# Scan products of a hybrid encoder: x stationary in half of the array, the decay matrix moving, the result transposed back

## The chip, the core and the metric

The kernel runs on one core of a Trainium2 chip, as one launch. The metric is the device time of that launch in microseconds (us), the median of several runs. A profiled execution gives the trace that is read here. TensorE is called PE in the rows, its weight loads PEld, VectorE DVE, ScalarE ACT, GpSimd POOL, and SyncE, which issues the DMAs, SP.

## What is computed

Two layers of an encoder over 256 positions of width 1024. Each layer has three parts: a mixer with three branches (dilated window attention, a state-space scan in both directions, a Fourier mix) whose outputs are gated, summed and projected; cross-attention into 256 memory tokens; and a SwiGLU feed-forward. The change touches the scan. Per head, with 32 heads of 64 channels in 4 groups, the reference has in essence

```
a_cs   = cumsum(dt * a)                              # per head, over positions
lmat   = exp(where(tri, a_cs[l] - a_cs[s], -inf))    # decay from s to l
cb     = einsum('bclgn,bcsgn->bcgls', C, B)
y_diag = einsum('bcgls,bcgels,bcsgep->bclgep', cb, lmat, x * dt)
y      = y_fwd + y_bwd + x * d_skip
```

For each head the diagonal part is a matrix over positions (cb times decays, both directions) times that head's x, 64 columns wide.

## The kernel before

Weights stream from memory in pieces of 1 MB, in the order of a list (`ORDER` and what follows it). SP loads a piece, ACT rounds it to a high part `wh` (L327), DVE takes the rest `wl` (L328), and PE multiplies three products per weight tile (L357 to L359, 512 columns moving; L418 to L420, 256 columns moving). There are three buffers each of raw and split pieces. After a piece, `done()` splits the piece three further on, and `pump()` gives background tasks some credit.

All else is background: Python generators in seven lanes, in which each `yield` ends a step. A step's yielded number is its price in credit; `LATER` blocks its lane for four pumps, `SOON` for three; a tuple such as `4, 0` says how many 4 KB and 2 KB slots of on-chip memory must be free before the next step. `drain()` runs everything that is left. A scheduler then orders each engine's instructions.

The scan of a group is `ssd_group`: two tiles (`tt`, 128 positions each) of eight heads. A tile fetches the cumulative sums of both directions from memory, spread over all partitions (`s<-dd`), builds `E` for eight heads (L841, L842, L848) and the weights `W` (L844, L845), multiplies them (L852), and scales x into `Xo` and `Xo2` (L862, L864). After `LATER` come eight products (L869) into the bank `pd`, with one head's 128x128 block of `E` stationary and 64 columns of x moving, and one product `po` (L870) for the other half of the positions. DVE adds and scales (L872 to L874), and the slots of `E` come free. With 2 layers, 4 groups and 2 tiles there are 16 such tiles, so 128 instructions at L869. The scan's output is then gated and normed (`ssd_gate`) and transposed (L907).

The list order is: Fourier, B and C columns, x, q, k, v, z columns mixed with gate columns, the attention branch (token BA, which waits for the attention lane), the last gate columns (G1), then `drain()`, then the projection of the scan's output (`branch(fl(yT), 4, ...)`), which uses group 0's output first and group 3's last.

Of the kernel before, what the change touches and what calls it, by code (L numbers as in the profile page):

```python
# [17 lines left out]
P = 128  # L18
# [15 lines left out]
LATER, SOON = "later", "soon"  # L34
# [141 lines left out]
def trunk(ctx: ExitStack, tc: tile.TileContext, a, out):  # L176
    nc = tc.nc
    V, A, T, G = nc.vector, nc.scalar, nc.tensor, nc.gpsimd
# [19 lines left out]
    def slot(size, shape, dt):  # L198
        keep = 0 if running[0] else RESERVE
        while len(slots[size]) <= keep and step():  # L200
            pass
        if not slots[size]:
            raise RuntimeError(f"no slot of {size} KB")
        r = slots[size].popleft()
        t = r.tile(shape, dt, name=nm("s%d_" % size))
        owner[id(t)] = (size, r, t)
        return t

    def s4(shape, dt=F32):
        return slot(4, shape, dt)  # L210

    def s2(shape, dt=F32):
        return slot(2, shape, dt)

    def free(*ts):
        for t in ts:
            if isinstance(t, (tuple, list)):
                free(*t)
            else:
                size, r, _ = owner.pop(id(t))  # L220
                slots[size].append(r)
# [4 lines left out]
    def banks_of(pool, n, p):  # L226
        banks = deque(pool.tile([P, 512], F32, name=f"{p}{i}") for i in range(n))

        def f():
            banks.rotate(-1)  # L230
            return banks[-1]
        return f

    tp = banks_of(pst, 4, "tp")
# [15 lines left out]
    def step(only=None, force=True):  # L250

        if running[0]:
            return False
        for k in (list(turn) if only is None else [only]):
            q = lanes[k]
            if blocked[k] and not force or need[k][0] > len(slots[4]) or need[k][1] > len(slots[2]):
                continue
            need[k] = (0, 0)
            while q:
                running[0] = True  # L260
                try:
                    c = next(q[0])
                except StopIteration:
                    q.popleft()
                    continue
                finally:
                    running[0] = False
                if isinstance(c, tuple):
                    need[k] = c
                elif c in (LATER, SOON):  # L270
                    blocked[k] = WAIT if c is LATER else NWAIT if k == "n" else XWAIT
                    if not force:
                        break
                else:
                    credit[0] -= c
                turn.remove(k)
                turn.append(k)
                return True
        return False
# [11 lines left out]
                raise RuntimeError("a background task waits for slots")  # L291

    def drain():
        while step():
            pass
        if any(lanes.values()):
            raise RuntimeError("a background task waits for slots")
        credit[0] = 0.0
# [53 lines left out]
    def ordered():  # L352

        return tc.manual_schedule(engines={mybir.EngineType.PE})
# [75 lines left out]
    def const(name, shape, src, dt=F32, eng=None):  # L430
        t = cp.tile(shape, dt, name=name)
        (eng or nc.sync).dma_start(t, src)
        return t
# [4 lines left out]
    idn = const("idn", [P, P], a["c_idn"])  # L438
# [382 lines left out]
    def ssd_group(l, g, xT, R, Dbc, ys):  # L821

        dt, nacs, wof, el = R["dt"], R["nacs"], R["wof"], R["el"]
        cbd, off = R["cb", g]
        yield 1, 0
        y = ys[g] = s4([P, 2, 512])
        for tt in range(2):
            yield 4, 0
            bcs = []
            for hf in range(2):  # L830
                b = s4([P, 4, 2, P])
                nc.sync.dma_start(b, bass.AP(tensor=R["dd"].tensor,
                                             offset=R["dd"].offset + (8 * g + 4 * hf) * 512 + tt * P,
                                             ap=[[0, P], [512, 4], [S, 2], [1, P]]))
                bcs.append(b)
            E = s4([P, 8, P])
            W = s4([P, 8, P])
            for j in range(8):
                hf = 8 * g + j
                b = bcs[j // 4][:, j % 4]  # L840
                A.activation(E[:, j, :], b[:, 1, :], AF.Identity, bias=nacs[:, tt, 32 + hf:33 + hf])  # L841
                V.scalar_tensor_tensor(E[:, j, :], b[:, 0, :], nacs[:, tt, hf:hf + 1], E[:, j, :],  # L842
                                       op0=ALU.add, op1=ALU.min)
                A.activation(W[:, j, :], cbd[:, tt, 0, :], AF.Copy, scale=dt[:, tt, hf:hf + 1])  # L844
                V.scalar_tensor_tensor(W[:, j, :], cbd[:, tt, 1, :], dt[:, tt, 32 + hf:33 + hf], W[:, j, :],  # L845
                                       op0=ALU.mult, op1=ALU.add)
                if j % 4 == 3:
                    A.activation(E[:, j - 3:j + 1, :], E[:, j - 3:j + 1, :], AF.Exp)  # L848
                    yield 1.6
            for hf in range(2):  # L850
                hs = slice(4 * hf, 4 * hf + 4)
                V.tensor_mul(E[:, hs, :], E[:, hs, :], W[:, hs, :])  # L852
            free(bcs, W)
            yield 1.1

            d = 1 - tt
            sl = slice(8 * g, 8 * g + 8)
            v8 = lambda t: t.rearrange("p (a b) -> p a b", a=8)
            bc8 = lambda t: t[:, :, None].to_broadcast([P, 8, 64])
            yield 0, 2  # L860
            Xo = s2([P, 512])
            V.tensor_mul(v8(Xo), v8(xT[:, 1 - tt, :]), bc8(wof[:, d, sl]))  # L862
            Xo2 = s2([P, 512])
            V.tensor_mul(v8(Xo2), v8(xT[:, tt, :]), bc8(Dbc[:, sl]))  # L864
            yield 1.2
            yield LATER
            pd, po = tp(), tp()
            for j in range(8):
                T.matmul(pd[:, j * 64:(j + 1) * 64], E[:, j, :], xT[:, tt, j * 64:(j + 1) * 64], start=True, stop=True)  # L869
            T.matmul(po, off[:, tt, :], Xo, start=True, stop=True)  # L870
            yt = y[:, tt, :]
            V.tensor_add(yt, Xo2, pd)  # L872
            V.tensor_mul(v8(Xo), v8(po), bc8(el[:, tt, sl]))
            V.tensor_add(yt, yt, Xo)  # L874
            free(E, Xo, Xo2)
            yield 1.8
        free(cbd, xT)
        if g == 3:
            free(R["off"])
# [132 lines left out]
    for l in range(L):  # L1012
# [104 lines left out]
        for n, tok in enumerate(ORDER):  # L1117
            k, g = tok[0], int(tok[1]) if tok[1].isdigit() else 0
# [20 lines left out]
            elif k == "x":  # L1139
                xT = s4([P, 2, 512])  # L1140
# [19 lines left out]
            elif tok == "BA":  # L1160
                drain_until(lambda: "oT" in R and R.get("a"), "a")
                branch(fl(R["oT"]), 1, ga)
                free(R["oT"], ga)
        free(h)
        drain()
        mT = ftiles(2)

# [312 lines left out]
```

## Time and profile before

| what | us |
|---|---|
| median of 3 runs | 1613.19 (1612.34 to 1613.2) |
| the profiled execution's own time | 1612.18 |
| its span, first to last instruction | 1610.1 |
| PE busy | 1592.1 |
| weight loads busy | 1381.0 |
| DVE busy | 1163.8 |
| ACT busy | 956.5 |

The profiled execution took 2.1 us outside the span of its instructions. A matmul in full 32-bit floats leaves two records in the trace, each with its own weight load; a transpose or a matmul on rounded operands (fp32r) leaves one. The time from one record's start to the next's (the pitch) tells what a matmul costs in a stream; its recorded duration holds the latency as well, which overlaps with the next.

### The profile page before, as it was taken

Reading aid. Unit: us, or ns where it says so; the run is one execution under the profiler, and the core shown is the slowest. Engines: PE = TensorE matmul, PEld = TensorE weight load, DVE = VectorE, ACT = ScalarE, POOL = GpSimd, SP = SyncE. Lnnn points to the kernel's source line nnn. Section 1 sums busy time; section 2 is a strip of 40 time slices with the busy share of each in tenths; the row PEclk is TensorE's granted clock in tenths of the full one; section 3 lists DMA queues with packets and bytes.
Section 4 is the critical chain, followed back from the end, with each engine's and each line's share of the span. In section 5 each row is a group of like instructions: output and inputs, shape, how many; then the busy total and the mean of one; then the engine's idle time right before and its main releaser. Section 6 shows DMA issues by size and latency. Waiting matters only on the chain.

```text
span 1610.1 us, 22777 instructions
## 1 busy us (share of the span) xinstructions
PE 1592.1 (99%) x8994; PEld 1381.0 (86%) x8994; DVE 1163.8 (72%) x1777; ACT 956.5 (59%) x1587; POOL 43.8 (3%) x47
## 2 busy tenths in 40 slices
PE   8999999999999999999999999999999999999999
PEld 6998888888887888999889888888888878889997
DVE  5999997889757566555478999978886576565543
ACT  5666868787445664444356678677964457554442
POOL 0000000000000100000000000000100001000000
PEclk9999999999999999999999999999999999999999
DMA  8446655455556444555554577455555545345552
GB/s 298 159 161 230 223 182 181 167 196 192 196 196 223 177 153 162 198 183 184 183 190 146 182 230 242 154 189 179 172 185 203 202 181 196 131 169 175 183 190 95
DMA packets 84579, 299.46 MB, mean 186 GB/s; under 512 B 7305, under 2 KB 46857, under 8 KB 52728
## 3 DMA queue, kind: packets, MB, share of 16 engines
q1 hardware_dynamic: 84472, 298.01, 52.8%
q8 instruction: 70, 1.15, 0.3%
q14 instruction: 37, 0.30, 0.1%
HBM read 296.77 MB, written 1.22 MB: 185 GB/s over the span
## 4 chain that ended last, share of the span: by engine, by line
PE 91%; DVE 4%; ACT 2%; DMA 1%; POOL 1%; issue 1%; SPq 0%; DVEq 0%; ACTq 0%; POOLq 0%
PE acc L358 20%; PE acc L357 20%; PE acc L359 20%; PE acc L418 7%; PE acc L419 7%; PE acc L420 7%; PE tp L869 1%; PE tp L477 1%; PE tp L357 1%; PE tp L359 1%; PE tp L358 1%; PE tp L619 1%; DVE wl L328 1%; PE tp L940 1%; ACT wh L327 1%; PE tp L870 1%
## 5 line engine op out<-in xcount | busy, mean ns | idle before, releaser
L328 DVE TENSOR_TENSOR wl<-wr,wh 128x2048 fp32r<-128x2048 f32 (+1 forms) x256 | 572.6, 2239 | 278.5 <-ACT wh L327 277.9
L327 ACT CAST wh<-wr 128x2048 fp32r<-128x2048 f32 (+1 forms) x256 | 477.6, 1867 | 387.8 <-PE acc L359 184.3
L357 PE MATMUL acc<-wh,s 128*128 128x512 f32 x1520 | 604.4, 398 | 0.1
L358 PE MATMUL acc<-wl,s 128*128 128x512 f32 x1520 | 599.6, 395 | 1.6 <-DVE wl L328 1.6
L359 PE MATMUL acc<-wh,s 128*128 128x512 f32 x1520 | 596.2, 393 | 0.0
L358 PEld LDWEIGHTS acc<-wl,s 128*128 128x128 f32 x1520 | 288.0, 189 | 61.7 <-DVE wl L328 3.9
L357 PEld LDWEIGHTS acc<-wh,s 128*128 128x128 f32 x1520 | 287.9, 189 | 59.3 <-issue 1.4
L359 PEld LDWEIGHTS acc<-wh,s 128*128 128x128 f32 x1520 | 287.8, 189 | 58.0 <-issue 0.4
L418 PE MATMUL acc<-s,wh 128*128 128x256 f32 x960 | 273.3, 285 | 0.0
L419 PE MATMUL acc<-s,wh 128*128 128x256 f32 x960 | 271.7, 283 | 0.0
L420 PE MATMUL acc<-s,wl 128*128 128x256 f32 x960 | 271.6, 283 | 0.0
L418 PEld LDWEIGHTS acc<-s,wh 128*128 128x128 f32 x960 | 184.1, 192 | 1.1 <-issue 0.7
L419 PEld LDWEIGHTS acc<-s,wh 128*128 128x128 f32 x960 | 184.2, 192 | 0.8 <-issue 0.5
L420 PEld LDWEIGHTS acc<-s,wl 128*128 128x128 f32 x960 | 184.1, 192 | 0.0
L710 DVE SCALAR_TENSOR_TENSOR s<-s,cw,s 128x254 f32<-128x254 f32 (+2 forms) x288 | 120.9, 476 | 0.3
L841 ACT ACTIVATE s<-s,nacs 128x128 f32<-128x128 f32 x128 | 46.4, 392 | 13.4 <-DVE s L852 5.6
L844 ACT ACTIVATE s<-s,dt 128x128 f32<-128x128 f32 x128 | 45.3, 394 | 0.0
L842 DVE SCALAR_TENSOR_TENSOR s<-s,nacs,s 128x128 f32<-128x128 f32 x128 | 42.4, 344 | 3.5 <-ACT s L841 3.5
L845 DVE SCALAR_TENSOR_TENSOR s<-s,dt,s 128x128 f32<-128x128 f32 x128 | 41.5, 343 | 0.0
L493 DVE TENSOR_TENSOR s<-tp,s 128x512 fp32r<-128x512 f32 x56 | 36.9, 683 | 5.3 <-ACT s L492 5.2
L1199 DVE TENSOR_TENSOR X<-X,acc 128x512 f32<-128x512 f32 x24 | 16.4, 684 | 27.9 <-PE acc L359 27.9
L461 ACT ACTIVATE s<-X 128x512 f32<-128x512 f32 x24 | 15.1, 630 | 35.6 <-DVE X L1199 33.4
(224 smaller groups left out, 1418.8 us busy)
## 6 DMA issues: line engine op xcount, KB each, us to landing
wr<-in_wstream SPq DMA_DIRECT2D x248, 1024.0 KB, 4.8
s<-dd SPq DMA_DIRECT2D x32, 512.0 KB, 5.1
s<-in_wstream SPq DMA_DIRECT2D x6, 512.0 KB, 3.3
s<-vd SPq DMA_DIRECT2D x12, 256.0 KB, 5.9
wr<-in_wstream SPq DMA_DIRECT2D x8, 256.0 KB, 5.3
s<-in_ssd_norm_g SPq DMA_DIRECT2D x8, 256.0 KB, 3.2
s<-in_memT SPq DMA_DIRECT2D x4, 512.0 KB, 6.4
X<-in_x SPq DMA_DIRECT2D x2, 512.0 KB, 3.6
```

Of the source, the lines that this page charges most:

```text
L327: A.copy(hi[:, c], raw[:, c])
L328: V.tensor_sub(lo[:, c], raw[:, c], hi[:, c].bitcast(F32))
L357: T.matmul(o, sh, mh, start=start, stop=False)
L358: T.matmul(o, sh, ml, start=False, stop=False)
L359: T.matmul(o, sl, mh, start=False, stop=stop)
L418: T.matmul(o, hi[:, w0:w0 + P], sh[:, k, :], start=kt == 0, stop=False)
L419: T.matmul(o, hi[:, w0:w0 + P], sl[:, k, :], start=False, stop=False)
L420: T.matmul(o, lo[:, w0:w0 + P], sh[:, k, :], start=False, stop=kt == npk - 1)
L710: V.scalar_tensor_tensor(v[:, b, i0:i1], u[:, b, i0 + k - 3:i1 + k - 3], c[:, k:k + 1], v[:, b, i0:i1], op0=ALU.mult, op1=ALU.add)
L841: A.activation(E[:, j, :], b[:, 1, :], AF.Identity, bias=nacs[:, tt, 32 + hf:33 + hf])
L842: V.scalar_tensor_tensor(E[:, j, :], b[:, 0, :], nacs[:, tt, hf:hf + 1], E[:, j, :], op0=ALU.add, op1=ALU.min)
L844: A.activation(W[:, j, :], cbd[:, tt, 0, :], AF.Copy, scale=dt[:, tt, hf:hf + 1])
```

## The change

The eight products of a tile exchange their operands: 64 columns of x are stationary, and the 128 columns of a head's `E` move. The result of a head is transposed, 64 channels by 128 positions. An even head writes to partitions 0 to 63 of the bank and the odd head beside it to partitions 64 to 127, so that two heads fill a 128x128 block. In the built program these 128 instructions use half of the array: tile size 128x64, positions 0 and 64 in turn. ACT copies the bank to a new 2 KB tile `yf`, `E` is freed there, the task yields with `SOON`, and four transposes bring the blocks back into `pd`. `drain()` tries a second time before it gives up.

```
     def drain():
-        while step():
+        while step() or step():
             pass
...
             yield LATER
+            yield 0, 1
+
+            pf = tp()
+            with ordered():
+                for j in range(8):
+                    T.matmul(pf[64 * (j % 2):64 * (j % 2) + 64, j // 2 * P:(j // 2 + 1) * P],
+                             xT[:, tt, j * 64:(j + 1) * 64], E[:, j, :], start=True, stop=True)
+            yf = s2([P, 512])
+            A.copy(yf, pf)
+            free(E)
+            yield 0.0
+            yield SOON
             pd, po = tp(), tp()
-            for j in range(8):
-                T.matmul(pd[:, j * 64:(j + 1) * 64], E[:, j, :], xT[:, tt, j * 64:(j + 1) * 64], start=True, stop=True)
+            for k in range(4):
+                T.transpose(pd[:, k * P:(k + 1) * P], yf[:, k * P:(k + 1) * P], idn)
             T.matmul(po, off[:, tt, :], Xo, start=True, stop=True)
             yt = y[:, tt, :]
             V.tensor_add(yt, Xo2, pd)
             V.tensor_mul(v8(Xo), v8(po), bc8(el[:, tt, sl]))
             V.tensor_add(yt, yt, Xo)
-            free(E, Xo, Xo2)
+            free(yf, Xo, Xo2)
```

In the kernel after, the products are L872, the copy L875, the transposes L881, the other product L882, and the three DVE operations L884 to L886; everything behind them has moved by 12 lines.

On PE, the first scan tile of layer 0 before (`s_126` is x, `s_196` is `E`, `tp` a bank):

```order
L420 MATMUL acc_118<-s_8_136,wl_1597 128x256
L869 MATMUL tp_111<-s_126_968,s_196_1643 128x64 x8
L870 MATMUL tp_112<-s_198_1681,s_167_1371 128x512
L418 MATMUL acc_115<-s_6_134,wh_1626 128x256
L419 MATMUL acc_115<-s_7_135,wh_1626 128x256
```

The same tile now, at the same place and some 60 rows further on (`s_210` is `yf`):

```order
L420 MATMUL acc_118<-s_8_136,wl_1597 128x256
L872 MATMUL tp_111<-s_196_1643,s_126_968 64x128 x8
L418 MATMUL acc_115<-s_6_134,wh_1626 128x256
...
L359 MATMUL acc_116<-wh_1711,s_7_135 128x512
L881 MATMUL tp_114<-idn,s_210_1806 128x128 x4
L882 MATMUL tp_111<-s_198_1681,s_167_1371 128x512
L357 MATMUL acc_117<-wh_1711,s_6_134 128x512
```

The products stand where they stood; the transposes and the other product form a second group among the weight products.

On PE, the third scan tile of layer 0 now, between attention products (L619) of the same stage:

```order
L619 MATMUL tp_112<-s_260_2332,s_272_2376 128x256
L872 MATMUL tp_113<-s_257_2275,s_203_1717 64x128
L619 MATMUL tp_111<-s_260_2332,s_269_2368 128x256
L872 MATMUL tp_113<-s_257_2275,s_203_1717 64x128
L619 MATMUL tp_112<-s_260_2332,s_272_2376 128x256
L872 MATMUL tp_113<-s_257_2275,s_203_1717 64x128 x6
```

Eight products that stood in one run (L869 x8 before) now come in three. Over the program L872 comes in 26 runs for its 16 tiles.

On PE, where layer 0's last gate columns end and the scan's projection begins, before (`s_387` is group 0's output):

```order
L359 MATMUL acc_115<-wh_4156,s_9_137 128x512
L907 MATMUL tp_113<-idn,s_367_3348 128x128 x4
L907 MATMUL tp_114<-idn,s_367_3348 128x128 x4
L357 MATMUL acc_116<-wh_4190,s_387_3538 128x512
L358 MATMUL acc_116<-wl_4191,s_387_3538 128x512
```

The same place now (`s_464` is the last tile's `E`, `s_380` group 0's output):

```order
L359 MATMUL acc_115<-wh_4140,s_9_137 128x512
L872 MATMUL tp_114<-s_464_4231,s_301_2713 64x128 x8
L882 MATMUL tp_112<-s_469_4287,s_167_1371 128x512
L357 MATMUL acc_116<-wh_4201,s_380_3481 128x512
L358 MATMUL acc_116<-wl_4202,s_380_3481 128x512
L359 MATMUL acc_116<-wh_4201,s_381_3482 128x512
...
L881 MATMUL tp_111<-idn,s_474_4336 128x128 x4
```

The last tile of the last group has moved from some 280 rows ahead of this place to the place itself; its transposes stand six weight products behind.

On ACT at the same place now, ahead of the copy L875 that these transposes read (L1055 is the tanh of the gate columns, L904 the square of the gated output):

```order
L327 CAST wh_4281<-wr_4110 128x2048
L904 ACTIVATE s_476_4347,gst_4349<-s_426_3921 128x512
L1055 ACTIVATE s_450_4112<-s_450_4112 128x512
L327 CAST wh_4319<-wr_4144 128x2048
L1055 ACTIVATE s_451_4113<-s_451_4113 128x512
L875 COPY s_474_4336<-tp_114 128x512
```

The copy is queued behind a weight rounding and two tanh.

## Rows read from the trace of the kernel before

**Rows 1.** The page, part 1: busy time, share of the span, instructions.

```profile
PE 1592.1 (99%) x8994; PEld 1381.0 (86%) x8994; DVE 1163.8 (72%) x1777; ACT 956.5 (59%) x1587; POOL 43.8 (3%) x47
```

**Rows 2.** Windows of 40 us: stretch, length, each engine's busy us, clock, DMA share.

```profile
160.00:200.00 40.00, 39.93 (x237) 34.99 (x236) 38.71 (x74) 32.29 (x76) 0.00 (x0) 1.00 0.66 212
320.00:360.00 40.00, 39.16 (x209) 32.28 (x208) 34.83 (x81) 34.57 (x90) 3.60 (x2) 1.00 0.56 191
360.00:400.00 40.00, 39.20 (x211) 32.30 (x211) 37.33 (x92) 29.85 (x64) 0.73 (x1) 1.00 0.54 189
```

**Rows 3.** Waits of PE, longest first: us in total, times, longest.

```profile
PE tp L525 <- ACT s L518: 7.8, 1, 7.8
...
PE acc L358 <- DVE wl L328: 1.6, 2, 0.8
PE tp L907 <- DVE s L674: 1.4, 2, 0.7
```

**Rows 4.** The chain that ended last, around the second scan tile: start, us, what.

```profile
198.53 0.23 PE acc L359
198.77 1.73 PE tp L869 x16
200.50 0.91 PE tp L870 x2
```

**Rows 5.** Line 869 on PE: records, ns min/median/max, first and last start, forms.

```profile
L869 PE MATMUL tp<-s,s x256: 217/275/323, 172.7 to 1177.9; 128*128 128x64 f32 x128
```

**Rows 6.** Timeline at the dt columns (64 stationary columns, 256 moving): start, us, engine.

```profile
54.99 0.28 PE L419 MATMUL acc<-s,wh 128*128 128x256 f32 x1
55.12 0.28 PE L1078 MATMUL acc<-s,s 128*64 128x256 f32 x1
55.12 0.13 PEld L1079 LDWEIGHTS acc<-s,s 128*64 128x64 f32 x1
55.23 0.28 PE L1079 MATMUL acc<-s,s 128*64 128x256 f32 x1
...
57.62 0.28 PE L1079 MATMUL acc<-s,s 128*64 128x256 f32 x1
...
57.73 0.28 PE L420 MATMUL acc<-s,wl 128*128 128x256 f32 x1
```

**Rows 7.** Timeline at the cumulative sums (32 stationary columns at L770).

```profile
75.33 0.36 PE L756 MATMUL tp<-la,tri 128*128 128x32 f32 x2
...
75.53 0.39 PE L757 MATMUL tp<-la,tri 128*128 128x32 f32 x2
...
75.84 1.06 PE L770 MATMUL tp<-tri,la 128*32 128x128 f32 x8
76.83 0.97 PEld L940 LDWEIGHTS tp<-s,s 128*128 128x128 f32 x8 [0.20 <-issue]
```

**Rows 8.** PE timeline around a split scan tile and around four transposes.

```profile
332.00 1.23 PE L869 MATMUL tp<-s,s 128*128 128x64 f32 x10
333.03 0.48 PE L359 MATMUL acc<-wh,s 128*128 128x512 f32 x1
333.35 1.02 PE L870 MATMUL tp<-s,s 128*128 128x512 f32 x2
...
335.60 0.60 PE L654 MATMUL tp<-idn,s 128*128 128x128 f32 x4
335.96 0.48 PE L357 MATMUL acc<-wh,s 128*128 128x512 f32 x1
336.27 0.39 PE L358 MATMUL acc<-wl,s 128*128 128x512 f32 x1
```

**Rows 9.** Line 655, an ACT copy of a whole bank: ns min/median/max.

```profile
L655 ACT COPY s<-tp x16: 558/574/606, 260.6 to 1172.1; 128x512 f32<-128x512 f32 x16
```

**Rows 10.** DVE where layer 0's last gate columns end.

```profile
443.90 0.69 DVE L1042 TENSOR_TENSOR s<-acc,s 128x512 f32<-128x512 f32 x1 [0.56 <-PE acc L359]
```

**Rows 11.** ACT at the same place.

```profile
443.94 1.90 ACT L327 CAST wh<-wr 128x2048 fp32r<-128x2048 f32 x1
445.75 0.62 ACT L1043 ACTIVATE s<-s 128x512 f32<-128x512 f32 x1
```

## The prediction, made before the changed kernel was run

> **What bounds the kernel now.** I read the page's first part, then the windows of 40 us, then PE's waits, then the chain and the timeline around the scan. The first view shows PE busy for 1592.1 of 1610.1 us, with DVE at 72% and ACT at 59% [rows 1]. The windows tell whether that holds in the stages where the scan runs: at 160 to 200 us PE is busy for 39.93 of 40 us although DVE is nearly full too, and at the end of the scan it still has 39.16 and 39.20 [rows 2]. The waits say what is missing: 7.8 us once at the start, then 1.6 and 1.4 us in two waits each, one of each kind per layer, where the attention branch waits for its lane [rows 3]. So PE's stream sets the time: an instruction added to PE lengthens the kernel by its pitch, and one added to ACT or DVE costs only where PE then waits for it.
>
> **What the products cost before.** In the chain a tile's eight products are 16 records and take 1.73 us, 0.108 us each [rows 4]. They move only 64 columns, and a record's duration of 275 ns [rows 5] is mostly latency. Weight products with 256 columns moving follow each other at about the same pitch, 0.12 us (54.99 to 55.12, [rows 6]), so before the change the load of 128 stationary columns sets the pitch, not the 64 columns that move.
>
> **The change part by part.**
>
> *Products, one head after the other.* The new form has 64 stationary columns and moves 128 full 32-bit columns in two records. The trace has the first property in the dt columns: 22 steps from 55.12 to 57.62 us, 0.1136 us each, with a load of 0.13 us [rows 6]. The second it has at L770: eight records with 128 columns moving take from 75.84 to 76.83 us with an idle 0.20 us at the end, about 0.10 each [rows 7]. If the halves of the array took turns, a tile would cost 16 x 0.1136 = 1.82 us: nothing saved.
>
> *Products, two heads at once.* No row of before has two halves at work together, so this cost has to be bounded. A head's two records use the same half and must follow each other; the second can run beside the first record of the next head. Eight heads then take nine steps instead of 16, 9 x 0.1136 = 1.02 us, and 0.71 us less than before; 16 tiles give -11.4 us. The upper end is the 1.82 us above (+1.4 us). I take nine steps, because the program gives neighbouring heads different halves and because the loads in the rows already run ahead under the products of others.
>
> The Trainium skill, "TensorEngine Tiling (Array Packing)", Performance Considerations, advises just this swap for 64 moving columns and gives up to twofold for it. No run here shows it yet; by it the sum is the one of the forecast.
>
> *Transposes.* Four transposes push the next weight product from the usual 0.23 us [rows 4] to 0.67 us (335.60 to 336.27, [rows 8]), so a group of four costs 0.44 us with what it takes to get the weight stream going again (0.31 us for the first product behind it instead of 0.23). Since the transposes share their place with L882 and the products now stand alone, exactly one such group is new per tile: 16 x 0.44 = +7.0 us.
>
> *Runs that are broken up.* L872 comes in 26 runs for 16 tiles. One product squeezed into a tile costs 0.32 us instead of 0.23 (333.03 to 333.35, [rows 8]), and each break loses one overlapped step of 0.11: ten breaks x 0.20 = +2.0 us. L881 and L882 are broken eight times and L869 and L870 were as well, which cancels.
>
> *Going into half of the array and out again.* At width 64 the dt columns show nothing: 0.13 us in and 0.11 out (57.62 to 57.73), the usual pitch [rows 6]. At width 32 with full 32-bit operands the entry takes 0.31 us for two records where 0.20 is usual, and the exit leaves 0.20 us idle [rows 7]. So a run costs between 0 and 0.31 us; I take 0.05, near the row of the same width: 26 x 0.05 = +1.3 us, with ends 0 and 8.
>
> The Trainium skill, same page, Key Properties, says that a change of tiling mode drains TensorE, which speaks against this change. The dt columns disagree, the 32-column run agrees in part; what a full drain would come to is a rival below.
>
> *Copies.* 16 copies of a bank at 0.574 us are 9.2 us of ACT [rows 9]. While the scan runs ACT has 5 to 10 us free in each 40 [rows 2] and PE does not wait for it, so they are hidden, except where transposes follow the copy closely. There is one such place per layer: the last tile. Before, its products stood some 280 rows ahead of the scan's projection; the new steps with their `SOON` delay each tile, and it now stands at the drain itself, with six weight products before its transposes. From the last gate product on, PE has 1.02 us of products, 0.86 of L882 with 0.08 for the restart, and 6 x 0.23: 3.3 us. ACT has a tanh that waits for DVE's read of the bank (0.69 [rows 10], then 0.62), a rounding of 1.90, a second tanh of 0.62 [rows 11] and the copy of 0.57: 4.4 us, and some 0.1 for handing over. PE waits about 1.2 us, in two layers +2.4 us, with ends 0 (DVE and ACT get there early) and 6 (another weight split of DVE in front). Behind the transposes DVE's three operations and the gate have 24 weight products, 5.5 us, of room, and group 3's output is not needed until 75 products after the drain. The other tiles have some 40 to 110 rows between copy and transposes.
>
> *What costs nothing.* DVE has the same operations on the same sizes. The slot that `yf` takes is small and `E` comes free earlier. The second try in `drain()` issues nothing. The DMAs are the same in number and size; those of the last tile move with it into a stretch with more room.
>
> **The sum**, against the profiled execution's 1612.2 us: -11.4 + 7.0 + 2.0 + 1.3 + 2.4 = +1.3 us, or 1613.5 us. The median of the runs lies 1.0 us above that execution, which makes it 1614.5 us. A measurement of this kernel can tell about 0.2%, 3.2 us, from no change, so this is no change.
>
> **The rivals.**
>
> *The halves take turns (slower).* Place: the 16 products of L872. Nothing in the trace shows two matmuls that overlap by more than latency, and all dt products, which use half 0 alone, keep the full pitch [rows 6]. Against it speaks only the form of the program. Price: products +1.4, transposes +7.0, breaks without lost overlap 10 x 0.09 = 0.9, entry and exit 1.3, and since PE comes to the last transposes 0.8 us later a wait of only 0.4 per layer, 0.8: +11.4, or 1624.6 us. It decides as soon as a tile's products take more than about 1.3 us.
>
> *All small terms fall away (faster).* Steps of 0.107 us make the products 0.96 and the gain 12.3 us; entry, exit and the wait at the drain are nothing; and with the last tile moved out of the way the waits of 3.0 us at the attention branch [rows 3] go. -12.3 + 7.0 + 2.0 - 3.0 = -6.3, or 1606.9 us. For it speaks that the end of the scan is where ACT and DVE are crowded [rows 2]; against it that three things must come together.
>
> *Every entry and exit waits until the array is empty.* A matmul's 275 ns [rows 5] less its pitch of 0.11 is 0.17 us of tail, twice in each of 26 runs: 8.8 us instead of 1.3, or 1622.0 us with the halves side by side. For it speaks the run at width 32 [rows 7], against it the one at width 64 [rows 6].
>
> **How the numbers follow.** I give the forecast 0.46, turns 0.30, small terms gone 0.15, full drain 0.09. Forecast alone: 1610.8 us without entry, exit and wait, up to 1619 with a wait of 3 us per layer and entry and exit at 0.08. The range 1607 to 1626 leaves out about half of the faster case and of the slow case the part above it, 0.15 together. Faster by over 0.2%: 0.13 of the faster case and 0.05 of the forecast, 0.18. Within 0.2%: 0.33 of the forecast and 0.02 of the faster case, 0.35. Slower: 0.30 + 0.09 + 0.08 = 0.47.
>
> **What would show it.** The chain or timeline of a tile at L872: 1.0 us for 16 records with starts in pairs says two at once, 1.8 says turns. The step from the last weight product into L872 and from it to the next one shows entry and exit. L881 in fours at about 0.44 us with the restart. PE's waits should have a new line, L881 on ACT L875, of about 1.2 us in two waits at the drain; many such waits elsewhere would say that the copies are not hidden. Busy time of ACT up by some 9 us, of DVE unchanged. The prediction is wrong if the products fall below 0.9 us a tile, if they take more than 1.3, or if PE loses over 3 us at a drain.

## The result and the profile after

The changed kernel takes 1629.41 us (median of 4 runs, 1627.56 to 1631.63), the kernel before in the same session 1612.82 us (4 runs, 1612.34 to 1613.20). The ratio is 1.010, with a 95% interval of 1.0088 to 1.0112: slower by 1.0%, 16.6 us. The forecast was 1614.5 us and no change, with a range up to 1626, so the prediction was wrong in its verdict and in its range. A second session gave 1629.13 us for the same kernel.

The profiled execution took 1628.38 us, its span 1626.3 (before 1610.1). From the page's first part, of after:

```profile
PE 1596.7 (98%) x9058; PEld 1375.2 (85%) x9058; DVE 1165.3 (72%) x1777; ACT 970.0 (60%) x1607; POOL 42.2 (3%) x47
```

PE is busy 4.6 us longer than in [rows 1], so busy time explains little of 16.2 us of span. The waits of PE, of after (us in total, times, longest):

```profile
PE tp L525 <- ACT s L518: 9.9, 1, 9.9
PE tp L795 <- DVE s L715: 5.2, 4, 2.2
PE tp L607 <- DVE s L493: 3.4, 2, 1.7
PE acc L357 <- ACT s L492: 2.3, 2, 1.2
...
PE acc L357 <- ACT s L495: 1.3, 1, 1.3
PE tp L919 <- DVE s L910: 1.1, 2, 0.5
```

Against [rows 3], L795 (the convolution's transposes), L607 (attention's q) and L357 behind L492 (attention's output) are new, 10.9 us in eight waits, and so are the 1.3 us at L357 behind L495. Of the two in [rows 3] that come once per layer, the 1.6 us at L358 are gone, and L907 (now L919) waits 1.1 us instead of 1.4, for another line. No line shows L881 waiting for the copy L875. The wait at the start (L525) was 7.8 us in the profiled execution of before and lies between 7.8 and 10.7 in all profiled executions, the unchanged program's among them.

The first of the windows in [rows 2], of after (busy us of PE, PEld, DVE, ACT and POOL, then PE's granted clock, DMA share, GB/s):

```profile
160.00:200.00 40.00, 37.78 (x220) 32.56 (x219) 36.92 (x68) 29.92 (x72) 0.00 (x0) 0.96 0.67 218
```

Between 160 and 200 us PE loses 2.2 of its 40 us, and its granted clock is 0.96 on average where it was full. What happens there is seen in PE's timeline of after (start, us from first start to last end, engine, line; in brackets the idle time before and what ended it):

```profile
174.59 0.28 PE L420 MATMUL acc<-s,wl 128*128 128x256 f32 x1
174.80 1.09 PE L872 MATMUL tp<-s,s 128*64 128x128 f32 x16
175.82 0.39 PE L418 MATMUL acc<-s,wh 128*128 128x256 f32 x1
176.05 0.28 PE L419 MATMUL acc<-s,wh 128*128 128x256 f32 x1
...
184.47 0.60 PE L881 MATMUL tp<-idn,s 128*128 128x128 f32 x4
184.90 1.02 PE L882 MATMUL tp<-s,s 128*128 128x512 f32 x2
...
189.07 0.94 PE L795 MATMUL tp<-idn,s 128*128 128x128 f32 x4 [2.22 <-DVE s L715]
189.66 0.78 PE L358 MATMUL acc<-wl,s 128*128 128x512 f32 x1
190.23 0.63 PE L359 MATMUL acc<-wh,s 128*128 128x512 f32 x1
...
192.76 0.39 PE L359 MATMUL acc<-wh,s 128*128 128x512 f32 x1
...
238.72 1.02 PE L619 MATMUL tp<-s,s 128*128 128x256 f32 x4
239.68 0.43 PE L872 MATMUL tp<-s,s 128*64 128x128 f32 x2
240.04 0.70 PE L619 MATMUL tp<-s,s 128*128 128x256 f32 x2
240.67 0.43 PE L872 MATMUL tp<-s,s 128*64 128x128 f32 x2
```

The tile itself takes the time that was forecast: 16 records of L872 from 174.80 to the next product at 175.82, 1.02 us instead of the 1.73 of [rows 4]. The transposes take 0.43 us (184.47 to 184.90). The loss comes afterwards. At 189.07 PE has stood 2.22 us for L715, and the weight products behind it follow each other at 0.43 us instead of 0.23 until 192.76: the granted clock is 0.5 there for 3.4 us, 1.2 GHz instead of 2.4.

The chain of waits, of after, from 174 to 191 us (start, us, what the time went to):

```profile
174.19 8.80 DMA s<-dd
...
183.02 0.03 ACT s L841
...
184.30 1.80 ACT wh L327
...
186.12 2.29 DVE wl L328
188.41 0.61 DVE s L715
...
189.07 0.94 PE tp L795 x4
190.01 0.43 PE acc L358
```

It begins with the third tile's fetch of cumulative sums (L832). ACT's first read of it, L841, stands in ACT's queue ahead of a weight rounding (L327) and a tanh of the convolution; so these, then DVE's L328 and L715, and then PE's L795 all come late. SP's timeline tells why the fetch is late; first of before, then of after:

```profile
166.91 0.99 SPq L832 DMA_DIRECT2D s<-dd  x2
...
171.84 1.04 SPq L554 DMA_DIRECT2D s<-vd  x2
```

```profile
168.93 2.50 SPq L554 DMA_DIRECT2D s<-vd  x4
173.80 0.34 SPq L317 DMA_DIRECT2D wr<-in_wstream  x1
174.19 2.10 SPq L832 DMA_DIRECT2D s<-dd  x2
```

The added step changed the order of the lanes. Before, two of the attention's bias fetches (L554) came behind the scan's fetch; now all four stand together ahead of it, with a weight piece between, and it is issued 7.3 us later (2.1 us of that are the later start). ACT's waits for these fetches, of before and of after:

```profile
ACT s L841 <- DMA s<-dd: 5.2, 5, 1.4
```

```profile
ACT s L841 <- DMA s<-dd: 11.1, 6, 4.4
```

To split the 16.2 us of span I took each PE record's time to the next record's start, set idle time apart, and summed by group, in both traces. Products: 27.63 to 19.27 us, -8.4. Transposes: +6.8. Attention products L619, between which L872 of three tiles per layer are scattered: 11.84 to 15.91, +4.1. Weight products: 1413.35 to 1417.57, +4.2. All else: -2.1. Idle time without the start: 6.58 to 16.07, +9.5. Start: +2.1. So PE's own work rose by 4.6 us and its waiting by 9.5; half of the 3.4 us at half clock, an estimated 1.7 us, is in the weight products.

### The profile page after: what moved, and what is told of

It is laid out like the page before. It is cut to its first block, busy times and chain, and to the rows that moved or that the text cites. A ratio compares the mean times of both kernels' runs of the same rounds, so it can differ in the third digit from the quotient of the medians.

```text
span 1626.3 us, 22919 instructions
## 1 busy us (share of the span) xinstructions
PE 1596.7 (98%) x9058; PEld 1375.2 (85%) x9058; DVE 1165.3 (72%) x1777; ACT 970.0 (60%) x1607; POOL 42.2 (3%) x47
## 4 chain that ended last, share of the span: by engine, by line
PE 85%; DVE 6%; ACT 5%; issue 2%; DMA 1%; POOL 1%; SPq 0%; DVEq 0%; POOLq 0%; ACTq 0%
PE acc L359 18%; PE acc L357 18%; PE acc L358 18%; PE acc L418 6%; PE acc L419 6%; PE acc L420 6%; DVE wl L328 2%; ACT wh L327 2%; PE tp L619 1%; ACT s L566 1%; PE tp L477 1%; DVE s L710 1%; PE tp L357 1%; PE tp L872 1%; PE tp L664 1%
## 5 line engine op out<-in xcount | busy, mean ns | idle before, releaser
L328 DVE TENSOR_TENSOR wl<-wr,wh 128x2048 fp32r<-128x2048 f32 (+1 forms) x256 | 572.8, 2239 | 285.4 <-ACT wh L327 284.7
L327 ACT CAST wh<-wr 128x2048 fp32r<-128x2048 f32 (+1 forms) x256 | 477.5, 1867 | 376.1 <-PE acc L359 169.0
L357 PE MATMUL acc<-wh,s 128*128 128x512 f32 x1520 | 607.1, 399 | 3.6 <-ACT s L492 2.3
L358 PE MATMUL acc<-wl,s 128*128 128x512 f32 x1520 | 600.4, 395 | 0.0
L357 PEld LDWEIGHTS acc<-wh,s 128*128 128x128 f32 x1520 | 288.7, 190 | 62.8 <-ACT s L492 3.5
L358 PEld LDWEIGHTS acc<-wl,s 128*128 128x128 f32 x1520 | 288.8, 190 | 58.6 <-issue 2.5
L841 ACT ACTIVATE s<-s,nacs 128x128 f32<-128x128 f32 x128 | 47.1, 397 | 16.8 <-DMA s<-dd 11.1
L492 ACT CAST s<-tp 128x512 fp32r<-128x512 f32 x56 | 31.8, 589 | 19.5 <-PE tp L1344 5.1
L842 DVE SCALAR_TENSOR_TENSOR s<-s,nacs,s 128x128 f32<-128x128 f32 x128 | 41.5, 344 | 1.2 <-ACT s L841 1.1
L493 DVE TENSOR_TENSOR s<-tp,s 128x512 fp32r<-128x512 f32 x56 | 37.2, 685 | 6.8 <-ACT s L492 6.8
```

The costliest lines, as they stand in the source:

```text
L327: A.copy(hi[:, c], raw[:, c])
L328: V.tensor_sub(lo[:, c], raw[:, c], hi[:, c].bitcast(F32))
L357: T.matmul(o, sh, mh, start=start, stop=False)
L358: T.matmul(o, sh, ml, start=False, stop=False)
```

## The experiments

Each is set beside a run of the kernel before on the same chip (median 1612.6 to 1614.0 us). The line numbers are those of the changed kernel where no edit moves them.

**Do the two halves work at once?** The same products, with the even heads first:

```
-                for j in range(8):
+                for j in (0, 2, 4, 6, 1, 3, 5, 7):
```

> The changed kernel with the heads of a tile in the order 0, 2, 4, 6, 1, 3, 5, 7, so that neighbouring products use the same half of the array. If two halves work at once in the changed kernel (16 records in 0.87 us, as its timeline reads), the products now take 14 steps of 0.107 to 0.114 us or more, about 1.7 us a tile, and the kernel gets 0.7 x 16 = 11 us slower: about 1641 us. If the records only look closer together and the array works on one at a time, nothing changes: 1629 us.

1635.61 us (1633.30 to 1641.98), ratio 1.014 (1.0118 to 1.0161). A tile in PE's timeline of this run:

```profile
173.94 1.58 PE L872 MATMUL tp<-s,s 128*64 128x128 f32 x16
175.45 0.39 PE L418 MATMUL acc<-s,wh 128*128 128x256 f32 x1
```

1.51 us instead of 1.02, and 28.78 us of products in the kernel instead of 19.27. With neighbours in the same half the gain is gone; so in the changed kernel neighbouring heads do run side by side. This part of the forecast holds. The kernel got 6.2 us slower and not 11: the tile lost 0.49 us and not 0.7, and the waits shifted too (L795 3.1 us, L607 5.3).

**What are the products worth without the rest?** Only the swap, in the steps of before, without copy and transposes (so the output of the scan stands in the wrong layout):

```
-            yield 0, 1
...
-            yf = s2([P, 512])
-            A.copy(yf, pf)
-            free(E)
-            yield 0.0
-            yield SOON
-            pd, po = tp(), tp()
-            for k in range(4):
-                T.transpose(pd[:, k * P:(k + 1) * P], yf[:, k * P:(k + 1) * P], idn)
+            pd, po = pf, tp()
...
-            free(yf, Xo, Xo2)
+            free(E, Xo, Xo2)
```

> The kernel before with the swapped products alone: x stationary in half of the array, two heads side by side, but no copy and no transposes; DVE reads the bank as it is, so the scan's layout is left wrong. The steps are those of before. The timeline of the changed kernel puts a tile's products at 1.11 us with entry and exit (0.09 and 0.15 of that) against 1.73 before: 16 x 0.62 = 10 us faster, about 1603 us. If entering and leaving the half array costs more than the timeline shows, it stays within 3 us of 1613.

1609.17 us (1608.02 to 1609.92, 7 runs), ratio 0.9972 (0.9961 to 0.9983), 4.8 us faster. Products fall by 9.8 us to 17.81, but L619 rises by 1.3, the other product (L882 in the changed kernel) by 0.6, other work by 1.2 and idle time by 1.7. So the swap's own gain is half of the 9.8 us that its records show, and less than the 6.8 us of the transposes that it needs.

**What does the step cost without the swap?** The products of before, then the copy and the split step, without transposes:

```
-            pf = tp()
...
+            pd = tp()
+            for j in range(8):
+                T.matmul(pd[:, j * 64:(j + 1) * 64], E[:, j, :], xT[:, tt, j * 64:(j + 1) * 64], start=True, stop=True)
             yf = s2([P, 512])
-            A.copy(yf, pf)
+            A.copy(yf, pd)
...
-            pd, po = tp(), tp()
-            for k in range(4):
-                T.transpose(pd[:, k * P:(k + 1) * P], yf[:, k * P:(k + 1) * P], idn)
+            po = tp()
...
-            V.tensor_add(yt, Xo2, pd)
+            V.tensor_add(yt, Xo2, yf)
```

> The kernel before with its own products (E stationary, x moving), but with the changed kernel's steps: ACT copies the bank to a 2 KB tile, E is freed, the task yields with SOON, and the product po and DVE's three operations follow in the later step, DVE reading the copy. No transposes, no half of the array. If the loss comes from the steps and the order they make (theories 1 and 2), PE waits 10 us or more as in the changed kernel and the time is 1622 to 1627 us. If it comes from PE's new work (rival 3), it stays at 1612 to 1615 us.

1619.86 us (1615.86 to 1622.81, 7 runs), ratio 1.0029 (1.0018 to 1.0041). PE has hardly more to do, and the kernel pays 5 to 6 us, less than the 8 or more that the expectation put on the step. Its PE waits:

```profile
PE tp L795 <- DVE s L715: 4.8, 2, 3.0
PE tp L607 <- DVE s L493: 3.9, 2, 2.0
```

They are the two largest new waits of the changed kernel, with ACT waiting 12.6 us for the fetch at L841 and two stretches at half clock. The fetch of the third tile stands behind four bias fetches and a piece here too (SP issues it at 173.63 us). So these waits come with the step, not with the array.

**Is it the earlier release of E?** `E` freed where `yf` is freed:

```
-            free(E)
...
-            free(yf, Xo, Xo2)
+            free(E, yf, Xo, Xo2)
```

> The changed kernel, but E is freed with Xo and Xo2 at the tile's end, as it was before the change, not after the copy. Theory 1 (early release): the next tile's fetch of cumulative sums takes the slot of E, waits for the products, lands some 9 us late, and ACT stands in front of it; so without the early release the waits of PE at L795 (5.2 us in four) and the half-clock stretch of 3.4 us behind the first go, and the kernel comes to about 1621 us. Rival 2 (the split step itself, whatever is released): the waits move but stay, 1627 to 1631 us. Rival 3 (work on PE: transposes and entries into half the array): no change, 1629 us, with the same waits.

1626.10 us (1624.58 to 1628.51), ratio 1.0076 (1.0061 to 1.0091). L795 still waits 5.2 us, and ACT's longest wait at L841 is still 4.4. A half-clock stretch is there, but at 1162 us behind another wait (L872 on ACT's L582, 2.1 us). SP's queue has the order of the changed kernel, and the second half of the third tile's fetch still waits 1.2 us for L872. So the early release isn't what makes the fetch late. Its wait for the slot is still there, so what that wait is worth isn't shown by this run.

**Is it the step, or its delay?** First without `SOON`, then without either yield behind the copy (and with `E` freed at the end):

```
-            yield SOON
```

> The changed kernel with the first yield behind the copy but without SOON: the step is split, E is freed early, but the lane may go on at once. Theory 2 in its narrow form (the delay of three pumps per tile makes the harm): close to the version in one step, 1614 to 1618 us. If the split alone already upsets the order of the lanes, 1622 us or more.

```
-            free(E)
-            yield 0.0
-            yield SOON
...
-            free(yf, Xo, Xo2)
+            free(E, yf, Xo, Xo2)
```

> The changed kernel without the two yields behind the copy: products, copy, transposes and the other product in one step, E freed at its end, so that the background steps go as before the change. The swap, the copies and the transposes stay. Theory 2 (the loss beyond PE's own work comes from the split step): PE idles about as before, 6 to 9 us apart from the start, no half-clock stretch; products -9.8, transposes +6.8, what stands beside them +3 (read from the run with the products alone), one more group per tile +1: about 1614 to 1616 us. Rival 3 (work on PE and the copies): 1624 us or more, since all of that work is still there.

Without `SOON` 1621.16 us (1619.79 to 1622.30), ratio 1.0051 (1.0037 to 1.0065); in one step 1621.63 us (1619.76 to 1624.95), ratio 1.0053 (1.0039 to 1.0067). Both get about 8 us back. L795 no longer waits for L715, and the fetch goes out ahead of two of the bias fetches as before (SP issues it at 168.0 and 168.7 us). The waits that are left stand elsewhere; PE's of the run without `SOON`, then of the run in one step:

```profile
PE acc L357 <- ACT s L492: 3.5, 2, 1.8
PE tp L619 <- DVE s L620: 3.4, 3, 1.5
```

```profile
PE tp L619 <- DVE s L620: 8.2, 6, 2.4
```

I had expected the form in one step to cost a few us at most; it has 8 of its 14.5 us of idle time at the attention products instead, and two stretches at half clock.

**Can the fetch be brought forward?** Three tries. The scan's fetch on POOL's queue; the bias fetches there instead; and the bias fetches there without `SOON`:

```
-                nc.sync.dma_start(b, bass.AP(tensor=R["dd"].tensor,
+                nc.gpsimd.dma_start(b, bass.AP(tensor=R["dd"].tensor,
```

> The changed kernel with one word changed: the fetch of the cumulative sums (L832) is issued by POOL and not by SP, so it no longer stands behind bias fetches and a weight piece in SP's queue. PE's order is the same as in the changed kernel. If ACT's stand at L841 behind a late fetch is what makes PE wait at L795, ACT's wait for these fetches falls from 11.1 us to about 5, PE's wait at L795 from 5.2 us to under 2, the half-clock stretch goes, and the kernel comes to about 1624 us. If the fetch is late because its slot is still held by the products, or because weights take the bandwidth, little changes: 1627 to 1630 us.

```
-                nc.sync.dma_start(bt[:, :, b, :], bass.AP(tensor=vd.tensor, offset=vo + 256 * e,
+                nc.gpsimd.dma_start(bt[:, :, b, :], bass.AP(tensor=vd.tensor, offset=vo + 256 * e,
```

> The changed kernel, with one edit: the attention bias fetches (s<-vd, L554) are issued by POOL, so that on SP the third tile's fetch of cumulative sums (s<-dd, L832) no longer stands behind four of them and the first of its two halves goes ahead of a weight piece too. Theory A (ACT waits in its in-order queue at L841 for a fetch that starts too late, DVE's L715 then comes late, PE waits at L795 and its clock falls): ACT's wait at L841 near 183 and 988 us goes from 4.4 and 3.9 us to under 2, PE's waits at L795 (5.2 us) mostly go, the stretch at granted clock 0.5 goes, time 1622 to 1626 us against the changed kernel's 1629. Rival B (the waits at L795 come from the amount of ACT and DVE work in the stretch, not from the fetch): ACT's wait shrinks, but L795 keeps 4 to 5 us, time 1628 to 1631. Rival C (the second half, which waits for its slot until L872 is done, is the late one): L841 keeps 3 us or more and nothing changes, 1628 to 1631.

> The changed kernel without SOON and its price of 0.0 behind the copy (so that the transposes can come in the next step) and with the bias fetches issued by POOL. Without the bias edit this form took 1621.2 us and waited mostly for attention (L619 on DVE) and at the drain (L357 on ACT L492), while ACT's wait at L841 was short. Theory A: there is little late fetch left to mend, 1619 to 1622 us. Rival: bias fetches on SP were also in the way of the weight pieces, and their removal brings it below 1618; or POOL issues the bias late, and attention waits more, above 1624.

All missed. Of the first, ACT's waits and PE's:

```profile
ACT s L841 <- DMA s<-dd: 39.7, 14, 6.0
```

```profile
PE tp L881 <- ACT s L875: 8.3, 4, 3.8
PE tp L795 <- DVE s L715: 8.2, 4, 3.9
```

1647.70 us (1645.95 to 1648.44), ratio 1.0214 (1.0200 to 1.0228), with four stretches at half clock. The third tile's fetch went out no earlier: POOL issued its halves at 174.30 and 176.17 us, after waiting for their slots, and ACT read the first at 183.29. But the scheduler had also changed ACT's order: here L841 stands ahead of the copy L875 and a weight rounding, in the changed kernel behind them. So these wait as well, and with them the transposes L881. The edit changed two things, and its 18 us can't be put down to the queue.

The second took 1635.40 us (1631.86 to 1637.47), ratio 1.0142 (1.0126 to 1.0159). PE's longest wait after the start, then SP's and ACT's timeline of this run:

```profile
PE tp L795 <- DVE s L715: 9.2, 3, 5.0
```

```profile
169.18 0.38 SPq L832 DMA_DIRECT2D s<-dd  x1
173.03 0.33 SPq L317 DMA_DIRECT2D wr<-in_wstream  x1
175.17 0.38 SPq L832 DMA_DIRECT2D s<-dd  x1
```

```profile
175.45 0.99 ACT L841 ACTIVATE s<-s,nacs 128x128 f32<-128x128 f32 x3 [2.23 <-DMA s<-dd]
...
183.58 1.28 ACT L841 ACTIVATE s<-s,nacs 128x128 f32<-128x128 f32 x4 [3.11 <-DMA s<-dd]
```

The first half of the fetch did go out at 169.18. But here too the scheduler moved its readers: three of them now stand ahead of the rounding L327, which starts at 176.34 instead of 174.79, and ACT waits 2.23 us for the first half as well. The second half waited 1.8 us for its slot, until the products L872 had read it, was issued at 175.17, behind a piece, and ACT waited 3.11 us for that one (rival C of the expectation; that it would change nothing was wrong, the time rose by 6 us). So the bias fetches are not the whole reason for the lateness of the fetch: for its second half the slot is another, because the next tile's fetch now comes just behind the products that free it.

The third took 1631.40 us (1625.47 to 1631.95), ratio 1.0105 (1.0086 to 1.0124), 10 us more than without `SOON` alone. The wait that is new in it:

```profile
PE tp L880 <- ACT s L875: 7.7, 2, 4.5
```

The fetch goes out at 168.37 us, as without `SOON` alone (168.04), and ACT's order around its readers is the same; but ACT gets it at 178.49 instead of 174.22, and the copy behind it is late. Why it lands later isn't shown; attention (L619) waits 2.8 us and not longer than without this edit (3.4), so the expectation's reason for a slower run did not come true.

**Are the copies too much for ACT?** The copy on DVE:

```
-            A.copy(yf, pf)
+            V.tensor_copy(yf, pf)
```

> The changed kernel, with the 16 copies of the bank into yf done by DVE instead of ACT. Theory A (the late fetch blocks ACT's queue; the copy's engine matters little): ACT's wait at L841 near 183 us stays at 4 us and PE's at L795 at 4 to 6 us; time 1628 to 1632 us, within 3 us of the changed kernel. Rival B (the copies themselves crowd ACT and so make PE wait): ACT gains 9 us of room, PE's idle time falls by 4 us or more, 1622 to 1626. Rival C (DVE, at 72% and nearly full in the scan's stretches, is the one without room): 9 us more on DVE make PE wait longer at L795, L607 and L619, 1633 to 1640.

1637.09 us (1632.37 to 1637.68), ratio 1.0142 (1.0126 to 1.0159): 8 us slower than with the copies on ACT. PE's wait at L795 is 6.7 us, at L607 4.4. Taking the copies off ACT did not help, and DVE has less room. Theory A's wait stayed, but its time was too low; the extra belongs to rival C.

**Without the wait for the fetch.** L841 and L842 read a constant tile instead of the fetched sums, in the changed kernel and in the one before. All fetches are still issued, and only their readers are gone; `E` holds other numbers, and the scale keeps them finite:

```
-                A.activation(E[:, j, :], b[:, 1, :], AF.Identity, bias=nacs[:, tt, 32 + hf:33 + hf])
-                V.scalar_tensor_tensor(E[:, j, :], b[:, 0, :], nacs[:, tt, hf:hf + 1], E[:, j, :],
+                A.activation(E[:, j, :], tri[:, 1, :], AF.Identity, bias=nacs[:, tt, 32 + hf:33 + hf])
+                V.scalar_tensor_tensor(E[:, j, :], tri[:, 0, :], nacs[:, tt, hf:hf + 1], E[:, j, :],
...
-                    A.activation(E[:, j - 3:j + 1, :], E[:, j - 3:j + 1, :], AF.Exp)
+                    A.activation(E[:, j - 3:j + 1, :], E[:, j - 3:j + 1, :], AF.Exp, scale=0.001)
```

> The changed kernel, in which L841 and L842 read a constant tile instead of the fetched cumulative sums: the fetches are issued as ever, but nobody waits for them, so E holds other numbers. Theory A (ACT's in-order queue stands at L841 for the fetch, so DVE and then PE are late): ACT's waits for s<-dd (11.1 us) go, PE's waits at L795 (5.2 us) fall below 1.5 us, the stretch at granted clock 0.5 goes, time 1620 to 1624 us against 1629. Rival B (the split step leaves the lanes behind whatever the fetch does): ACT's waits go, but PE still waits 4 us or more at L795 or at places new to it, 1627 to 1631 us.

> The kernel before with the same edit: L841 and L842 read a constant tile, the fetches are issued as ever. ACT waits 5.2 us for them in the kernel before, and PE hardly at all (6.6 us of idle time, none at L795). Theory A: nothing on PE depends on it, 1611 to 1614 us, so that the two kernels differ by 8 to 11 us instead of 16.6. Rival B: the same time here, and the two still differ by 14 to 18 us. A third way: the fetch wait also holds the kernel before back, 1606 to 1609 us, and the difference stays for that reason.

The changed kernel then takes 1620.34 us (1619.16 to 1622.93), ratio to the kernel before 1.0046 (1.0031 to 1.0061). The kernel before, with the same edit, takes 1613.51 us (1611.75 to 1614.43), ratio 1.0002 (0.9992 to 1.0012). The window and PE's waits of the changed one:

```profile
160.00:200.00 40.00, 40.00 (x236) 34.64 (x235) 39.58 (x69) 31.81 (x77) 0.00 (x0) 1.00 0.71 229
```

```profile
PE tp L607 <- DVE s L493: 3.5, 2, 1.8
PE acc L357 <- ACT s L492: 2.3, 2, 1.2
```

PE is busy for all of the 40 us, its clock is full, and L795 does not wait at all, though SP's queue has the same order and the fetch goes out at 173.42 us. The wait for the fetch is worth about 9 us in the changed kernel and nothing in the one before. (The edit also lets the fetch's slots come free without a reader, and the scheduler moved a few instructions of ACT and DVE and one group of L795; what of the 9 us that makes was not separated.) The difference of the two falls from 16.6 to 6.8 us.

**The same kernel again.**

> The changed kernel once more, beside the others on the same chip, as their measure: 1627 to 1632 us, with PE's wait at L795 and a half-clock stretch again.

1629.13 us (1626.60 to 1630.51), ratio 1.0099 (1.0085 to 1.0113). The wait at L795 was 7.0 us here and 5.2 in the first profile; in this place single profiles differ by some 2 us, so only the larger differences above are read. The half-clock stretch is elsewhere: it follows a wait of 2.74 us at 510.69 us (L357 behind L495), while L795's waits of 3.04 and 2.17 us had none behind them. So it comes with PE's longer waits, but not always with the same one.

## Why the prediction was wrong

*The bound* was read rightly: PE sets the time, and everything that it lost can be found in its pitches and waits.

*Products.* Forecast 1.02 us per tile, measured 1.02: two heads do work side by side, and the rival of turns is refuted by the run with the even heads first. But nine steps were not what came. Record by record, the 16 start in eight pairs, the two of a pair 0.01 us apart; the second pair follows the first after 0.16 us and the others after 0.109 each. The next product comes 0.20 us after the last pair. So eight steps, 0.87 us, together with an entry and an exit came to the time of nine steps without them: the size is right in part by luck.

*Transposes.* Forecast 7.0, measured 6.8 us.

*Entry and exit* was mis-sized. Into the run the step is 0.21 us where 0.12 is usual (174.59 to 174.80), and the first step inside takes 0.16 instead of 0.11. The next product comes 0.20 us after the last record instead of 0.11 and is itself followed at 0.23 instead of 0.12 (175.82 to 176.05). Added up, a run pays some 0.34 us and not the 0.05 that I took from the dt columns [rows 6]. That is the price of the rival to which I gave 0.09, every entry and exit waiting until the array is empty (0.17 us twice). Over 26 runs it is an estimated 8.8 us instead of 1.3. The run of 32 columns in [rows 7] had shown it: its eight records start 0.113 us apart ((1.06 - 0.27) / 7, not 0.10), 0.31 us after two records that usually take 0.20, and the next product comes 0.20 us after the last. The Trainium skill ("TensorEngine Tiling (Array Packing)", Key Properties) says that a change of mode drains the engine; these rows agree with it for full 32-bit products, where the dt columns showed nothing. Why those show nothing stays open.

*Broken runs.* All ten breaks stand between attention products: in each layer three tiles come in three, three and two runs. In the versions with fewer runs (20 without `SOON`, 18 in one step) products take 17.8 and 17.7 us and L619 13.2 and 12.7; in the changed kernel 19.27 and 15.91. Scattering thus costs about 1.5 + 3 = 4.5 us, where breaks were forecast at 2.0. The rows from 238.72 show how: the two records of a head that stands alone cost 0.36 us there instead of 0.11, and two of L619 0.63 us instead of the 0.44 that such a pair takes in the kernel before (248.67 to 249.11).

*The copies at the drain.* Forecast: two waits of 1.2 us at L881. There were none. Of after, ACT and PE at that place, the drain of layer 0:

```profile
451.83 0.63 ACT L1055 ACTIVATE s<-s 128x512 f32<-128x512 f32 x1
452.36 0.57 ACT L875 COPY s<-tp 128x512 f32<-128x512 f32 x1
```

```profile
449.87 1.09 PE L872 MATMUL tp<-s,s 128*64 128x128 f32 x16
...
453.25 0.60 PE L881 MATMUL tp<-idn,s 128*128 128x128 f32 x4
```

PE takes 3.4 us from L872 to L881, about the 3.3 of the forecast, but the copy is done after 3.1 and not 4.4: the first of the two tanh runs at 449.45, while PE is still at the last gate product, and only the rounding, the second tanh and the copy are left. Two other waits of 1.2 us, 2.3 in all, came 35 us earlier in each layer: the attention branch's first product (L357 at 414.96) waits for ACT's L492, which rounds attention's output, transposed at 411.30 (before at 378.72). That has nothing to do with the copy, and that the sizes agree is chance.

*"What costs nothing"* is the step that failed. I wrote that the DMAs are the same in number and size and that the other tiles have 40 to 110 rows between copy and transposes. Both are true and neither helps: an added step changes the order of the lanes, and with it SP's and ACT's queues. The third tile's fetch went out 7.3 us later, ACT stood in order at its first reader, and PE paid at L795, a place that the change doesn't touch, and in the first profile with a stretch at half clock on top. That is about 9 us by the pair of runs without the fetch wait, where I had put nothing.

The other 6.8 us stand in the run without that wait. Its profile, summed by group as above and set against the profile of before, without the start: products -8.4, weight products +1.7, L619 +4.1, transposes +6.8, all else -2.4, idle time +4.5, together 6.3 us. Products with breaks, entries and exits (the first three) thus come to -2.6 us instead of the forecast -8.1. Idle time was forecast at +2.4, at the drain; what came is 3.5 us at L607, 2.3 at L357 behind L492 and 1.4 behind L495, less what went of the waits in [rows 3]. So the mis-sized entry, exit and breaks are the second step that failed, and waits at places that the sum left out the third.

What stays open: why L493 ahead of attention's q (L607) and the cross-attention's L495 are late after the change I did not follow to their first cause. How much of the fetch's lateness is its place behind the bias fetches and how much its slot was not separated either. None of the versions that compute the reference was faster than the kernel before.

## What to carry to other kernels

When a change splits a background step in two, compare the order on every queue before costing it, DMA queues first: find each fetch that moves behind another, and what stands in order behind its first reader. Compare again after each try at a cure: moving fetches to another queue made the scheduler move readers in ACT's queue as well, and the two tries of that kind cost 6 and 18 us. A swap that halves a product's time is worth it only if the result needs no transposing back: here 64-column halves gave 4.8 us, and the way back cost 6.8 us on PE before any wait. Price a run of half-array products with its entry and exit, here some 0.34 us, and by whether it stays whole; scattered pairs cost three times as much a record (0.18 us against 0.054).

## What the runs showed of the hardware

- Two full 32-bit products on different halves of the array, 64 stationary and 128 moving columns, do overlap: their records start in pairs, a pair every 0.109 us, where the 128-column form had one record every 0.108 [rows 4]; with the halves in sequence, 1.51 us a tile instead of 1.02.
- Such a run between products of the full array paid some 0.34 us for entry and exit together (0.09 + 0.05 + 0.09 + 0.11, above).
- After an idle time of 2.22 us PE was granted 0.5 of its clock (1.2 GHz) for 3.4 us, and weight products took 0.43 us instead of 0.23. The length of the wait alone does not tell when: in the second execution of the same kernel waits of 3.04 and 2.17 us were not followed by such a stretch and one of 2.74 was, and with the copies on DVE one of 1.85 was and one of 2.27 was not.
- A fetch of 512 KB issued at 175.17 us was read by ACT at 183.58, 8.4 us later, while weight pieces were under way (bias fetches on POOL). That POOL's queue is slower isn't shown: from issue to landing these fetches took 5.7 us in the median from POOL, and from SP 4.4 in the changed kernel and 6.2 in the run with the bias fetches on POOL.
